# Differential attention with score products over 128 rows, gate inputs moved to the last tiles, and half-width query factors in gated linear attention

## The chip, the cores and the metric

The kernel runs on one core of one Trainium2 chip. The metric is the device time in microseconds (us) from launch to end. The engines in the text are TensorE (PE, with its weight loads shown apart as PEld), VectorE (DVE), ScalarE (ACT), GpSimd (POOL) and SyncE (SP, which here only issues DMAs).

## The reference

Four mixers run one after the other on a sequence of 1024 positions and 1024 features: gated linear attention (GLA), a dilated sliding-window attention, differential attention (DA), and a latent attention (MLA). The change touches the first and the third.

In GLA (4 heads, 128 key and 256 value features per head) the attention inside a chunk is a product of queries and keys with a decay that depends on both positions:

```
diff  = bc[:, :, :, None, :] - bc[:, :, None, :, :]
decay = where(causal, exp(where(causal, diff, 0.0)), 0.0)
att   = einsum('bhid,bhjd,bhijd->bhij', qc, kc, decay)
```

In DA each of 8 heads has two score maps (c = 0, 1) with 64 features each, whose softmaxes are subtracted; the values have 128 features. The result is normalised, multiplied with a gate made from z (the "gate inputs", a quarter of the input projection) and projected:

```
sc = einsum('bqhcd,bkhcd->bhcqk', qb, k) * scale
p  = softmax(sc, axis=-1)
p  = p[:, :, 0] - lam * p[:, :, 1]
o  = einsum('bhqk,bkhd->bqhd', p, v)
...
o  = rmsnorm(o, subln_g) * (1.0 - lambda_init)
o  = o.reshape(b, s, DA_WIDTH) * silu(z)
return o @ w_out
```

## The kernel before

Products in full precision are made from three passes: each operand is split into a rounded part (hi) and a remainder (lo), and hi·hi, lo·hi and hi·lo are added in PSUM (the lines L165, L166 and L167 of one helper). Each product has 128x128 weights and up to 512 moving columns.

**Filler.** The independent projections are cut into *units* with *pieces*; a piece of the width met here is three products of 512 columns. A `Fill` object holds the queue. `fill.give(ns)` issues pieces at this place of the program until their estimated cost has used up the credit, `fill.need(tag)` issues until a unit is complete, `fill.keep` is the number of pieces that `give` must leave over, and what is left at the end of a stage (`self.left`) is issued in the boundary that follows. So the order on TensorE is fixed when the program is written; an engine waits in its own order.

**GLA.** `gla_core` runs over the 4 heads. For each level m in 64, 32, .. 1 the pairs of positions that straddle a block border of size m get their decay: VectorE writes the exponents e for both halves (L478, L479; 512 columns each), ScalarE applies exp to all 1024 columns, VectorE multiplies the keys (L482, tile `ktl`, two buffers) and the queries (L483, in place into e), and TensorE multiplies the two in 128x128 blocks (L495 for m below 64, L487 for m = 64; both in unsplit fp32, which the trace shows as two passes for each product). L496 copies the valid parts into `att` under a mask; then a `give` follows.

**DA.** The body runs over 64 tiles i of 128 queries (8 heads of 8 tiles). At tile i TensorE transposes the tile of j = i - 2 (`attend`, L1248), whose evacuation is split into PTh (ScalarE, L1250) and PTl (VectorE); then come the 8 score products of tile i (L1443, into the PSUM tile `sc` with two buffers, one for each c, both of two banks); then, after odd j, the norm of the pair of tiles before (L161), filler by `give`, and the value products `pv` of the pair (L1381, L1382, L1384; L1379 transposes the row sums). The two maps of a tile go through a maximum on VectorE (L1447) and an exp on ScalarE (L1449); `combine` (L1465 to L1467) subtracts them one tile later.

The operands of the scores are made by filler units `u_k` and `u_q` of the next head, with their rotation on GpSimd and VectorE. `QS[c]` holds the hi part of the queries in its 64 rows and the lo part in the other 64; `KH[c]` holds the hi part of the keys in both halves (L1346 by ScalarE, L1347 a second cast on GpSimd); `KL` holds lo parts. A product over all 128 rows (QS with KH) gives hi·hi + lo·hi; a product over 64 rows (QS with KL) gives hi·lo. The order is: for c = 0 both 128-row products, both 64-row ones; for c = 1 both 64-row ones, then both 128-row ones.

**Gate inputs.** `zs` holds 13 units of 8 pieces (a head and a half of the sequence each). Two are issued before the body, one is added at the start of each of the heads 0 to 6 and three at head 7; the last one is added behind the loop with keep = 8, so that its pieces stand in the boundary. There, per head and half of the sequence, `gated` loads z (L793), the attention output (L794) and the norm factors (L802) by SP's queue, and makes the left operands `oh` and `ol` of the output projection (L796 to L804).

Of the kernel before, what the change touches and what calls it, by code (L numbers as in the profile page):

```python
# [137 lines left out]
class Kern:  # L138
# [317 lines left out]
    def gla_core(self, gp, pp, fill, h, qT, kT, v, bs, masks, ahead):  # L456
# [14 lines left out]
        for li, m in enumerate(LEVELS):  # L471
# [11 lines left out]
            V.tensor_tensor(e, qT, e, op=OP.mult)  # L483
            if m == 64:
                pl = pp.tile([128, 8, 64], F32, name="lv")
                for c in range(8):
                    T.matmul(pl[:64, c, :], kt_[:, c * 128:c * 128 + 64], e[:, c * 128 + 64:c * 128 + 128], start=True, stop=True)  # L487
                V.tensor_copy(att[:64].rearrange("p (c i) -> p c i", i=128)[:, :, 64:128], pl[:64])
                fill.give(2200)
                continue  # L490
            for hf in range(2):
                pl = pp.tile([128, 512], F32, name="lv")
                for c in range(4):
                    cc = slice((4 * hf + c) * 128, (4 * hf + c) * 128 + 128)
                    T.matmul(pl[:, c * 128:c * 128 + 128], kt_[:, cc], e[:, cc], start=True, stop=True)  # L495
                V.copy_predicated(view(att[:, half(hf)])[:, :, 1, :],  # L496
                                  masks[:, li * 256:li * 256 + 256].rearrange("p (n m) -> p n m", m=m), view(pl)[:, :, 1, :])
# [755 lines left out]
    def factors(self, pool, hs):  # L1253
# [3 lines left out]
        t, e, y = (lambda x: (x[:, 0], x[:, 1], x[:, 2]))(pool.tile([128, 3, 4 * len(hs)], F32, name="vr"))  # L1257
# [23 lines left out]
    def da(self, before):  # L1281
# [3 lines left out]
        with ExitStack() as ctx:  # L1285
# [34 lines left out]
            QS, KH, KL, VH = {}, {}, {}, {}  # L1320

            def u_q(h):
                def pre():
                    QS[h] = [dp.tile([128, 1024], F32R, name=f"qs{c}", bufs=2) for c in range(2)]

                def evac(hf, s, ps):
                    def rest(t1, t2):
                        (G if h else V).tensor_tensor(t1, t1, t2, op=OP.add)
                        for c in range(2):
                            a, b = rows[c], rows[1 - c]  # L1330
                            S.copy(QS[h][c][a, s], t1[a])
                            self.lo(G if h else V, QS[h][c][b, s], t1[a], QS[h][c][a, s])
                    return self.rope(None, ps, C, Sn, s, self.SWAP64, rest, 0.125, ((dp, 2),) * 2 if hf else None)
                return self.u_t(("q", h), ("da_wq", h), evac, pre=pre)

            def u_k(h):
                def pre():
                    KH[h] = [dp.tile([128, 1024], F32R, name=f"kh{c}", bufs=2) for c in range(2)]
                    KL[h] = dp.tile([128, 1024], F32R, name="kl", bufs=2)

                def evac(hf, s, ps):
                    def rest(t1, t2):
# [462 lines left out]
```

## Time and profile before

| what | before |
|---|---|
| median of 3 runs (lowest to highest) | 2756.11 us (2754.12 to 2759.56) |
| the profiled execution | 2754.68 us |
| its span, first to last instruction | 2752.9 us |
| PE busy | 2651.4 us (96%) |
| DVE busy | 1873.2 us (68%) |
| ACT busy | 1337.4 us (49%) |
| POOL busy | 312.7 us (11%) |

The span is 1.8 us shorter than the profiled execution's own time; the rest lies around it. In the span the stages follow each other: GLA's cores lie between about 40 and 380 us, the body of DA between about 1470 and 1982 us, and the boundary between DA and MLA begins at about 1983 us. PE and PEld are the same engine: a weight load can run while the product before it still streams. A matmul's duration in the trace runs from its start to its modelled end and overlaps with the next; what a product costs in a stream is the distance between starts.

### The profile page before, as it was taken

To read this page: it belongs to the slowest core of one execution; us is meant where nothing else is said; L and a number is where in the kernel's file an instruction comes from. 1 tells how busy PE (TensorE), PEld (TensorE's weight loads), DVE (VectorE), ACT (ScalarE), POOL (GpSimd) and SP (SyncE) were. 2 spreads that over 40 slices of the span, in tenths; PEclk is the share of its full clock that TensorE was granted. 3 is DMA by queue.
4 is the path that set the end of the run, shared out by engine and by line. 5 is a ranking of instruction groups with operands and counts; after the bars stand their busy time and mean duration, and the time that the engine had idled before them with its cause. 6 is when DMAs were issued, how large, how long until landed. Compare 5 with 4: busy or idle time off the path is not lost.

```text
span 2752.9 us, 39334 instructions
## 1 busy us (share of the span) xinstructions
PE 2651.4 (96%) x14804; PEld 2232.2 (81%) x14804; DVE 1873.2 (68%) x3431; ACT 1337.4 (49%) x2530; POOL 312.7 (11%) x224
## 2 busy tenths in 40 slices
PE   8999999999999999989999999999899999999998
PEld 7889887887778878867787787777678788888878
DVE  7776637657666666666657878888776527777785
ACT  5543344415343434445615676666545424555562
POOL 0000000000000000000005666666100000000000
PEclk9999999999999999999999999999999999999999
DMA  5311146554111111154553222222375220100143
GB/s 207 108 41 37 47 149 205 202 190 147 51 50 47 41 48 47 57 175 158 193 195 90 58 60 69 63 68 54 97 278 173 75 76 24 30 28 30 38 174 111
DMA packets 155606, 274.70 MB, mean 100 GB/s; under 512 B 24564, under 2 KB 74068, under 8 KB 153752
## 3 DMA queue, kind: packets, MB, share of 16 engines
q1 hardware_dynamic: 155416, 272.19, 30.1%
q8 instruction: 116, 1.90, 0.3%
q14 instruction: 74, 0.61, 0.1%
HBM read 195.48 MB, written 66.17 MB: 95 GB/s over the span
## 4 chain that ended last, share of the span: by engine, by line
PE 70%; DVE 14%; DMA 7%; ACT 5%; issue 3%; SPq 1%; POOL 0%; DVEq 0%; ACTq 0%; POOLq 0%
PE mm L165 15%; PE mm L166 15%; PE mm L167 15%; PE pt L1248 3%; PE sc L1443 3%; PE sc L1681 2%; PE sc L1057 2%; PE lv L495 1%; DVE den L1447 1%; DVE P L1467 1%; PE pt L1161 1%; DVE wlo L150 1%; PE mm L1647 1%; PE sc L166 1%; ACT P L1449 1%
## 5 line engine op out<-in xcount | busy, mean ns | idle before, releaser
L165 PE MATMUL mm<-xh,whi 128*128 128x512 f32 x1456 | 611.2, 420 | 8.0 <-DVE t L919 4.3
L167 PE MATMUL mm<-xh,wlo 128*128 128x512 f32 x1456 | 573.5, 394 | 2.0 <-POOL wlo L150 2.0
L166 PE MATMUL mm<-xl,whi 128*128 128x512 f32 x1456 | 573.4, 394 | 1.7 <-DVE xl L150 1.7
L165 PEld LDWEIGHTS mm<-xh,whi 128*128 128x128 f32 x1456 | 276.9, 190 | 64.8 <-DVE t L919 5.6
L167 PEld LDWEIGHTS mm<-xh,wlo 128*128 128x128 f32 x1456 | 275.4, 189 | 62.8 <-POOL wlo L150 2.7
L166 PEld LDWEIGHTS mm<-xl,whi 128*128 128x128 f32 x1456 | 276.7, 190 | 52.6 <-DVE xl L150 4.1
L150 POOL TENSOR_TENSOR wlo<-wraw,whi 128x1024 fp32r<-128x1024 f32 x29 | 70.2, 2422 | 1322.1 <-ACT whi L192 1320.4
L165 PE MATMUL mm<-wvhi,xh 128*128 128x256 f32 x704 | 206.6, 293 | 6.2 <-DVE v L349 2.0
L192 ACT CAST whi<-wraw 128x1024 fp32r<-128x1024 f32 (+2 forms) x141 | 136.0, 964 | 135.9 <-PE mm L166 126.9
L167 PE MATMUL mm<-wvhi,xl 128*128 128x256 f32 x704 | 201.1, 286 | 0.0
L166 PE MATMUL mm<-wvlo,xh 128*128 128x256 f32 x704 | 200.7, 285 | 0.0
L1449 ACT ACTIVATE P<-sc,den 128x1024 f32<-128x1024 f32 x128 | 142.8, 1116 | 109.6 <-DVE den L1447 109.5
L150 DVE TENSOR_TENSOR wlo<-wraw,whi 128x1024 fp32r<-128x1024 f32 (+2 forms) x113 | 123.6, 1093 | 88.2 <-ACT whi L192 81.3
L1447 DVE TENSOR_REDUCE den<-sc 128x1 f32<-128x1024 f32 x128 | 153.0, 1211 | 0.7 <-PE sc L1443 0.7
L165 PEld LDWEIGHTS mm<-wvhi,xh 128*128 128x128 f32 x704 | 136.2, 194 | 11.5 <-ACT vs L1297 4.4
L1051 ACT ACTIVATE P<-P,nm 128x128 f32<-128x128 f32 (+1 forms) x192 | 84.9, 443 | 124.3 <-DVE nm L1049 124.0
L166 PEld LDWEIGHTS mm<-wvlo,xh 128*128 128x128 f32 x704 | 136.9, 194 | 1.0 <-issue 0.7
L167 PEld LDWEIGHTS mm<-wvhi,xl 128*128 128x128 f32 x704 | 136.2, 193 | 0.0
L165 PE MATMUL mm<-oh,xh 128*128 128x512 f32 (+1 forms) x336 | 126.0, 375 | 0.6 <-ACT oh L804 0.5
L166 PE MATMUL mm<-ol,xh 128*128 128x512 f32 (+1 forms) x336 | 123.9, 369 | 2.2 <-DVE ol L150 2.2
L167 PE MATMUL mm<-oh,xl 128*128 128x512 f32 (+1 forms) x336 | 123.4, 367 | 0.0
L1061 DVE CUSTOM_DVE_ANT_0 P<-sc,band 128x128 f32<-128x128 f32 (+1 forms) x192 | 59.6, 348 | 70.0 <-PE sc L1057 69.4
(352 smaller groups left out, 6086.2 us busy)
## 6 DMA issues: line engine op xcount, KB each, us to landing
xa<-in_ada_w SPq DMA_DIRECT2D x12, 2048.0 KB
d_z<-zt SPq DMA_DIRECT2D x64, 256.0 KB
oh<-d_z SPq DMA_DIRECT2D x64, 256.0 KB
ol<-d_o SPq DMA_DIRECT2D x64, 256.0 KB
d_r<-X SPq DMA_DIRECT2D x48, 256.0 KB
wraw<-in_swa_wq SPq DMA_DIRECT2D x24, 512.0 KB
res<-d_r SPq DMA_DIRECT2D x40, 256.0 KB
zt<-zt SPq DMA_DIRECT2D x160, 64.0 KB
```

The source lines that it names most:

```text
L150: eng.tensor_tensor(out, src, hi.bitcast(F32), op=OP.subtract)
L165: mm(ps, l[0], r[0], start=first, stop=False)
L166: mm(ps, l[0], r[1], start=False, stop=False)
L167: mm(ps, l[1], r[0], start=False, stop=last)
L192: nc.scalar.copy(hi, raw)
L1051: S.activation(p[:, off:off + w_], p[:, off:off + w_], AF.Exp, bias=nm[:, g, b:b + 1], scale=scale, accum_out=stat(h, g, 1, b))
L1057: T.matmul(sc[:, b % 2, :w_], q[:, b * 128:b * 128 + 128], k[:, k0:k0 + w_], start=True, stop=True)
L1061: V.tensor_tensor_reduce(p[:, off:off + w_], sc[:, b % 2, :w_], mk, 1.0, NEG, op0=OP.add, op1=OP.max, accum_out=stat(h, g, 0, b))
L1248: nc.tensor.transpose(pt[:, i, :], P[:, (4 * j + i) * 128:(4 * j + i) * 128 + 128], self.ident)
L1443: T.matmul(sc[c][:, s], QS[h][c][r, q0:q0 + 128], (KL[h] if k else KH[h][c])[r, s], start=first, stop=not first)
L1447: V.tensor_reduce(dn[:, 2 + c:3 + c], sc[c], AX, OP.max, negate=True)
L1449: S.activation(p, sc[c], AF.Exp, bias=dn[:, 2 + c:3 + c], accum_out=dn[:, 1:2] if c else d0)
```

## The change

In GLA the query factor is made only for the second half of each block, into a tile `eq` of 512 columns (two tiles, `khT` and `qh`, in turn), and a product has 64 moving columns in place of 128. One PSUM tile per level takes all eight products.

In DA `QH[c]` holds the hi part of the queries in both halves of the rows and `KK[c]` the keys' hi part in its 64 rows and lo part in the other 64. `QL` (a ring of three half tiles for each c, of which GpSimd clears the unused rows once) holds the lo part of the queries in 64 rows and zeros in the others. QH with KK gives hi·hi + hi·lo, QL with KK gives lo·hi. All eight products of a tile run over 128 rows. For keys two casts per half of the sequence on GpSimd are gone, for queries two casts on ScalarE are new. The value halves are split from a buffer of their own instead of `vr`, and the norm factors take a `kh` buffer.

The gate inputs are taken in another order; the body adds one unit at each even head and four at head 7, and the last three units (24 pieces) are added at j = 62 with keep = 11. The credits in the body change with it.

```diff
@@ gla_core
-            V.tensor_tensor(e, qT, e, op=OP.mult)
+            eq = gp.tile([128, 512], F32, name=("khT", "qh")[li % 2])
+            V.tensor_tensor(eq.rearrange("p (n m) -> p n m", m=m), view(qT)[:, :, 1, :], ev[:, :, 1, :], op=OP.mult)
...
+            pl = pp.tile([128, 512], F32, name="lv")
+            for c in range(8):
+                T.matmul(pl[:, c * 64:c * 64 + 64], kt_[:, c * 128:c * 128 + 128], eq[:, c * 64:c * 64 + 64], start=True, stop=True)
             for hf in range(2):
-                pl = pp.tile([128, 512], F32, name="lv")
-                for c in range(4):
-                    cc = slice((4 * hf + c) * 128, (4 * hf + c) * 128 + 128)
-                    T.matmul(pl[:, c * 128:c * 128 + 128], kt_[:, cc], e[:, cc], start=True, stop=True)
@@ da
+            QL = [[dp.tile([128, 512], F32R, name=f"ql{c}{i}") for i in range(3)] for c in range(2)]
+            for i in range(3):
+                for c in range(2):
+                    G.memset(QL[c][i].bitcast(F32)[rows[1 - c], :], 0.0)
... u_q
-                            S.copy(QS[h][c][a, s], t1[a])
-                            self.lo(G if h else V, QS[h][c][b, s], t1[a], QS[h][c][a, s])
+                            S.copy(QH[h][c][a, s], t1[a])
+                            self.lo(G if h else V, QL[c][(2 * h + hf) % 3][a, :], t1[a], QH[h][c][a, s])
+                            S.copy(QH[h][c][b, s], t1[a])
... u_k
-                            S.copy(KH[h][c][a, s], t1[a])
-                            (G if h else V).tensor_copy(KH[h][c][b, s], t1[a])
-                            self.lo(G if h else V, KL[h][a, s], t1[a], KH[h][c][a, s])
+                            S.copy(KK[h][c][a, s], t1[a])
+                            self.lo(G if h else V, KK[h][c][b, s], t1[a], KK[h][c][a, s])
... load_v
-                vr = dp.tile([128, 8, 128], F32, name="vr")
+                vr = vl.bitcast(F32)
...
-                  [(hf, h) for h in range(3, 8) for hf in range(2)]]
+                  [(hf, h) for h in range(3, 6) for hf in range(2)] + [(0, 6), (0, 7), (1, 6), (1, 7)]]
... the body
+                if j == 62:
+                    fill.add(*zs)
+                    fill.keep = 11
...
-                        for _ in range(1 if h < 7 else 3):
+                        for _ in range(4 if h == 7 else 1 - h % 2):
                             fill.add(zs.pop(0))
...
-                    for n, (c, hf, k) in enumerate(((0, 0, 0), (0, 1, 0), (0, 0, 1), (0, 1, 1), (1, 0, 1), (1, 1, 1), (1, 0, 0), (1, 1, 0))):
-                        mm(c, hf, k, (c, hf) not in seen)
+                    scores(0)
+                    exps(0)
+                    scores(1)
...
-                    fill.give(4000 if j > 55 else 4200 if j > 7 else 4250)
+                    fill.give(4500 if j > 61 else 3200 if j > 55 else 4000 if j > 7 else 4250)
                 elif j >= 0 and j % 2:
-                    fill.give(2200 if j > 55 else 2300 if j > 7 else 2040)
+                    fill.give(4500 if j > 61 else 1700 if j > 55 else 2200 if j > 7 else 2040)
...
-            fill.keep = 8
-            fill.add(*zs)
+            fill.give(2500)
             norm(*nrm)
```

**TensorE at the last two score tiles.** The rows are in program order: line, operation, target from its two sources (kh, kl: keys; qs, ql: queries; the number is a buffer), shape and count. Before:

```order
L1384 MATMUL mm<-PTl,vh 128x256 x8
L1248 MATMUL pt<-ident,P 128x128 x8
L1443 MATMUL sc<-kh_16598,qs_16607 128x512 x2
L1443 MATMUL sc<-kl,qs_16607 128x512 x2
L1443 MATMUL sc<-kl,qs_16608 128x512 x2
L1443 MATMUL sc<-kh_16599,qs_16608 128x512 x2
L1248 MATMUL pt<-ident,P 128x128 x8
```

With the change, in the same place, the first of the filler pieces that now follow the eight products included:

```order
L1393 MATMUL mm<-PTl,vh 128x256 x8
L1250 MATMUL pt<-ident,P 128x128 x8
L1457 MATMUL sc<-kh_16498,qs_16506 128x512 x2
L1457 MATMUL sc<-kh_16498,ql_12401 128x512 x2
L1457 MATMUL sc<-kh_16499,qs_16507 128x512 x2
L1457 MATMUL sc<-kh_16499,ql_12404 128x512 x2
L165 MATMUL mm<-xh_70,whi 128x512
L166 MATMUL mm<-xl_72,whi 128x512
L167 MATMUL mm<-xh_70,wlo 128x512
```

The products of c = 0 and c = 1 stand in the same order of keys (hi with lo, then again), and five pieces stand before the next transposes, where none stood.

**TensorE behind the last scores.** Before, from the value products of the last pair but one to those of the last:

```order
L1384 MATMUL mm<-PTl,vh 128x256 x8
L1248 MATMUL pt<-ident,P 128x128 x8
L161 MATMUL mm<-sq_17838,ones_r 128x256
L161 MATMUL mm<-sq_17839,ones_r 128x256
L1248 MATMUL pt<-ident,P 128x128 x8
L1379 MATMUL mm<-ident,dsum 4x128
```

With the change, up to the first piece there:

```order
L1393 MATMUL mm<-PTl,vh 128x256 x8
L1250 MATMUL pt<-ident,P 128x128 x8
L161 MATMUL mm<-sq_17764,ones_r 128x256
L161 MATMUL mm<-sq_17765,ones_r 128x256
L165 MATMUL mm<-xh_70,whi 128x512
L166 MATMUL mm<-xl_72,whi 128x512
L167 MATMUL mm<-xh_70,wlo 128x512
```

Seven pieces now stand between this norm and the last transposes and seven more between those and the last value products; behind the last norm stand 11 pieces, where 8 stood. Counted over the whole stage, 332 pieces are issued in either kernel; up to tile i = 60 it is 304 before and 277 with the change, and at the tiles 61 to 65 it is 0, 0, 0, 0, 0 before and 2, 5, 3, 7, 7 with the change.

## Rows read from the trace of the kernel before

**Rows 1.** The page, busy time: engine, us, share of the span, instructions.
```profile
PE 2651.4 (96%) x14804; PEld 2232.2 (81%) x14804; DVE 1873.2 (68%) x3431; ACT 1337.4 (49%) x2530; POOL 312.7 (11%) x224
```
**Rows 2.** Windows: length, each engine's busy us, clock, DMA share, GB/s.
```profile
1480.00:1968.00 488.00, 480.53 (x2699) 382.39 (x2698) 401.44 (x492) 330.70 (x631) 283.08 (x200) 1.00 0.22 62
1949.00:1991.40 42.40, 31.46 (x173) 24.94 (x171) 28.34 (x60) 23.96 (x49) 2.80 (x3) 0.92 0.27 76
1991.40:2016.00 24.60, 22.11 (x80) 16.90 (x81) 22.93 (x48) 14.04 (x21) 0.00 (x0) 0.86 1.03 367
```
**Rows 3.** Timeline of PE in GLA: start, us, operation, count [idle before].
```profile
59.81 1.15 PE L487 MATMUL lv<-e,ktl 128*64 128x64 f32 x16
313.81 1.95 PE L495 MATMUL lv<-e,ktl 128*128 128x128 f32 x16
```
**Rows 4.** Timeline of weight loads in the sliding-window stage.
```profile
704.77 0.58 PEld L1117 LDWEIGHTS sc<-xb,sel 128*128 128x128 f32 x4 [3.72 <-DVE xb L1108]
```
**Rows 5.** Line L483: its durations (ns), and who waited for it (us, times).
```profile
L483 DVE TENSOR_TENSOR e<-qT,e x28: 1211/1216/1255, 55.0 to 337.5; 128x1024 f32<-128x1024 f32 x28
...
  PE lv L495: 5.8, 6
```
**Rows 6.** Groups in 1480 to 1968 us: busy us, mean ns, idle before.
```profile
L1347 POOL CAST kh<-zt 64x512 fp32r<-64x512 f32 x28 | 22.3, 798 | 1.5
L1331 ACT CAST qs<-zt 64x512 fp32r<-64x512 f32 x28 | 17.3, 616 | 9.7 <-POOL zt L1328 9.4
L1447 DVE TENSOR_REDUCE den<-sc 128x1 f32<-128x1024 f32 x127 | 151.9, 1211 | 0.7 <-PE sc L1443 0.7
L1467 DVE SCALAR_TENSOR_TENSOR P<-P,den 128x1024 f32<-128x1024 f32 x63 | 101.3, 1608 | 2.1
L150 DVE TENSOR_TENSOR PTl<-pt,PTh 128x512 fp32r<-128x512 f32 x124 | 81.5, 679 | 6.1 <-ACT PTh L1250 6.1
```
**Rows 7.** Timeline of PE: two tiles' scores and what follows them; the first one's c = 1 waits.
```profile
1668.80 0.73 PE L1443 MATMUL sc<-kl,qs 64*128 64x512 f32 x2 [0.30 <-ACT P L1449]
...
1670.03 0.40 PE L161 MATMUL mm<-sq,ones_r 128*128 128x256 f32 x2
...
1944.80 0.71 PE L1443 MATMUL sc<-kh,qs 128*128 128x512 f32 x2
1945.44 0.74 PE L1443 MATMUL sc<-kl,qs 64*128 64x512 f32 x4
...
1946.67 0.39 PE L165 MATMUL mm<-xh,whi 128*128 128x512 f32 x1
```
**Rows 8.** Line L1443: idle time before it, until whom (us, times).
```profile
  ACT P L1449: 11.8, 18
```
**Rows 9.** Timeline of PE in MLA: a score block behind transposes.
```profile
2301.27 0.71 PE L1681 MATMUL sc<-kp,qp 128*128 128x512 f32 x2
...
2302.51 0.62 PE L1681 MATMUL sc<-kp,qp 128*128 128x512 f32 x2
```
**Rows 10.** Timeline of PE behind tile 61: waits, and one filler piece.
```profile
1957.73 1.07 PE L1248 MATMUL pt<-ident,P 128*128 128x128 f32 x8 [1.02 <-DVE den L1465]
...
1963.30 0.73 PE L1443 MATMUL sc<-kh,qs 128*128 128x512 f32 x2 [1.83 <-ACT P L1449]
...
1974.74 1.82 PE L1248 MATMUL pt<-ident,P 128*128 128x128 f32 x8 [1.50 <-DVE PTl L150]
...
1981.74 0.39 PE L161 MATMUL mm<-sq,ones_r 128*128 128x256 f32 x1 [1.36 <-ACT sq L154]
...
1982.77 0.39 PE L165 MATMUL mm<-xh,whi 128*128 128x512 f32 x1
...
1983.45 0.39 PE L165 MATMUL mm<-xh,whi 128*128 128x512 f32 x1
...
1991.40 0.50 PE L165 MATMUL mm<-oh,whi 128*128 128x512 f32 x1 [3.03 <-ACT oh L804]
```
**Rows 11.** The chain that ended last, in the boundary: start, us, what.
```profile
2002.54 6.11 DMA rsb<-d_rs
```

More of the change, by code (lines that the diff above doesn't have):

```diff
@@ L486, in gla_core @@
                 for c in range(8):
-                    T.matmul(pl[:64, c, :], kt_[:, c * 128:c * 128 + 64], e[:, c * 128 + 64:c * 128 + 128], start=True, stop=True)
+                    T.matmul(pl[:64, c, :], kt_[:, c * 128:c * 128 + 64], eq[:, c * 64:c * 64 + 64], start=True, stop=True)
                 V.tensor_copy(att[:64].rearrange("p (c i) -> p c i", i=128)[:, :, 64:128], pl[:64])
@@ L1436, in da, with scores @@
                     sc = [None] * 2
-                    def mm(c, hf, k, first):
-                        s = half(hf)
-                        if sc[c] is None:
-                            sc[c] = pp.tile([128, 1024], F32, name="sc", bufs=2)
-                        r = rows[c] if k else slice(0, 128)
-                        T.matmul(sc[c][:, s], QS[h][c][r, q0:q0 + 128], (KL[h] if k else KH[h][c])[r, s], start=first,
-                                 stop=not first)
+                    def scores(c):
+                        sc[c] = pp.tile([128, 1024], F32, name="sc", bufs=2)
+                        ql = QL[c][(2 * h + t // 4) % 3][:, t % 4 * 128:t % 4 * 128 + 128]
+                        for k in range(2):
+                            for hf in range(2):
+                                T.matmul(sc[c][:, half(hf)], ql if k else QH[h][c][:, q0:q0 + 128], KK[h][c][:, half(hf)], start=k == 0,
+                                         stop=k == 1)
                     def exps(c):
@@ L1450, in exps @@
                         P.append(p)
-                    seen = set()
-                    for n, (c, hf, k) in enumerate(((0, 0, 0), (0, 1, 0), (0, 0, 1), (0, 1, 1), (1, 0, 1), (1, 1, 1), (1, 0, 0), (1, 1, 0))):
-                        mm(c, hf, k, (c, hf) not in seen)
-                        seen.add((c, hf))
-                        if n == 3:
-                            exps(0)
+                    scores(0)
+                    exps(0)
+                    scores(1)
+                    done[0] = i + 1
                     if nrm and j % 2:
```

38 lines of the change are left out of this document (20 added, 18 removed).

## The prediction

> **What bounds the kernel now.** The page's busy times come first: TensorE is busy 96% of the span [rows 1], so time falls only where TensorE has less to issue, or where it now waits. The windows tell the three places apart [rows 2]. In the body of DA (1480 to 1968 us) it is busy 480.5 of 488.0 us at full clock, VectorE 401, ScalarE 331 and GpSimd 283: filler covers nearly every wait. From 1949 to the first product of the boundary at 1991.4 it is busy 31.5 of 42.4 us at a clock of 0.92. Here the filler has run out, and the list of TensorE's waits [rows 10] shows what it waits for: the chain exp, combine, transposes, split, value products, norm. In the boundary the DMAs are full (1.03, 367 GB/s), and the chain goes through a norm factor that arrives 6.1 us after its predecessor [rows 2, 11]. So filler in the body costs its full length, and in the tail only what it exceeds the waits by. My sum is made against the profiled execution, 2754.7 us; the median of the runs is 1.4 us above it, and I add that at the end.
>
> **GLA.** A level below 64 has 16 passes (eight products in two) which take 1.95 us [rows 3], 15 distances and one duration of 0.28 us, thus 0.11 us a pass. Halving the moving columns would halve that if the columns set the pace. They don't: in the sliding-window stage, four products with 32 moving columns and the same 128 weight columns have four weight loads in 0.58 us [rows 4], three distances of about 0.11 us and one load of about 0.25. So I cost the narrower products at nothing (bounds 0 and the gain of the last rival below). What goes is a wait: TensorE stood 5.8 us in 6 places for the query factor [rows 5], a VectorE operation of 1.22 us on 1024 columns. On 512 columns it takes about 0.68, which the 128x512 subtraction of PTl (0.68 us, the same engine and width) bears out [rows 6]. It is also written to a tile of its own, so that the next level's factor no longer stands behind this level's use of e. If only the shorter duration counted, 6 x 0.54 = 3 us would go, less where the exp then comes last; at best all 5.8 and the fringe. I take **-5.8** (-2 to -7). VectorE loses 28 x 0.54 = 15 us there, which elsewhere was cover.
>
> **DA's operands.** For keys 28 casts of 0.80 us leave GpSimd (22.3 us); for queries 32 casts of 0.62 us come to ScalarE, +20 us on 331 of 488 [rows 2, 6]. They are pieces of work for the next head, and filler covers waits of ScalarE while it lasts: 0 here, bound by rival two. The six clearings run on GpSimd ahead of the body, where it has nothing else. At the start of the body the split of weights and the first operands stand on VectorE and GpSimd; two casts less may shorten that by **-1** (-2 to 0). The load of values now goes to a buffer that the value products of the head before read last. If that made SP wait, the weight loads and the row exchange of the rotation behind it in SP's queue would wait too; it is issued at a head's fifth tile, more than 20 us after that last reader, so 0.
>
> **DA's scores.** The eight products of a tile take 1.87 us (1944.80 to 1946.67), in 45 of 64 tiles within 0.03 of that. The 64-row products of c = 0 and c = 1 run in pairs, four of them in the 0.74 us of one row [rows 7]. All the same eight cost eight times 0.23, for those before and behind stand 0.31 to 0.34 apart. With 128 rows throughout, MLA shows what a block behind transposes costs: five products in 1.24 us [rows 9], that is 0.31 for the first and 0.23 for each that follows. Eight then cost 0.31 + 7 x 0.23 = 1.93, +0.05 x 64 = +3.2. Against that stand the 18 waits for the buffer of c = 1 (the exp two tiles of scores before, 11.8 us) [rows 8]. In such a tile nothing overlaps, and the last four products take 1670.03 - 1668.80 = 1.23 us [rows 7]; in the new form 4 x 0.23 = 0.92. That is 0.31 x 18 = -5.6. Together **-2.4** (-6, where the waits go too, to +3, where the gain does not come).
>
> **Moved filler.** Counted from the program, 304 pieces stood up to tile 60 and 277 do now. A piece, three products, takes 1983.45 - 1982.77 = 0.68 us [rows 10], so the body loses 27 x 0.685 = -18.5, in full, since it is busy throughout. Of these, 24 (16.4 us) now stand at tiles 61 to 65, and three in the boundary, where TensorE waits 3.03 us in any case [rows 10]. The tail has 42.40 - 31.46 - 3.03 = 7.9 us of waits and runs at 0.92, which is 0.08 x 42.4 = 3.4 us of slow clock, 11.3 in all [rows 2]. Of the waits, those before the transposes (1.02, 1.50) and before the last scores (1.83) have pieces ahead of them now: 4.35 us. Those before the norms stay (1.36 is the longest), since no piece stands between the value products and the norm. The clock fell towards its lower level behind these waits; with them filled I count that time as won, 3.4. Absorbed 4.35 + 3.4 = 7.75, added 16.4: +8.6. Together -18.5 + 8.6 = **-9.9** (-13.4, where all 11.3 are absorbed, to -2, where nothing is).
>
> **The boundary and the body's thin places.** Eleven pieces instead of eight hold a weight buffer longer, so one more load of 512 KB falls into the stretch where the DMAs are full: 512 KB at 367 GB/s is 1.4 us [rows 2], **+1.4** (0 to +3). The credits leave three and no pieces, or five and none, at the tile pairs 14/15, 30/31 and 46/47. There VectorE has, for each of the two tiles, two maxima, a subtraction and two splits, 2 x 1.21 + 1.61 + 2 x 0.68 = 5.4 us [rows 6], 10.8 for the pair, against 10.5 to 12 of TensorE. I take **+1.5** (0 to +4).
>
> Sum: -5.8 - 1 - 2.4 - 9.9 + 1.4 + 1.5 = **-16.2**, which is 2738.5 against the profiled execution and 2739.9 against the median.
>
> **The rivals.** *The tail does not absorb.* VectorE is busy 28.3 and ScalarE 24.0 of the tail's 42.4 us; if their chain simply starts later by each piece, because transposes stand behind pieces in TensorE's order, the tail grows by all 16.4: 2739.9 + 7.8 = 2748. Against it: the pieces stand in front of waits on just that chain [rows 10]. *ScalarE's new casts delay the exps.* 32 x 0.62 = 20 us in full: 2760. For it, exps gate both `sc` buffers [rows 8]; against it, ScalarE is free for a third of the body [rows 2]. *Slower: weight loads come to light.* If a 128-row product behind a 128-row product with other weights waits for its load, as inside the old block (0.33 from start to start), a block costs 8 x 0.33 = 2.65: 64 x 0.77 = +49 and the -2.4 is lost, 2792. The kernel gets slower from a block of 1.88 + 13.8/64 = 2.09 us. MLA's five in 1.24 us speak against it [rows 9]. The Trainium skill would have it so (TensorE: Matmul & The Clock Gate, Part 3: Packing small matmuls): weight loads overlap a running matmul only where its row group differs, and 128-row products use all groups; MLA's rows do not agree with that. *GLA's products do halve.* A pass with 64 weight columns and 64 moving ones costs (1.15 - 0.14) / 16, about 0.06 us [rows 3]; were that the price here, 24 levels x 16 x 0.05 = 20 us more go: 2720. The Trainium skill says in the same page, section Back-to-back issue gap, that the distance follows the moving columns down to a floor, which speaks for it; its section on LDWEIGHTS lets the load follow the weight's columns, and our rows 4 are on that side.
>
> **How the numbers follow.** The forecast, 2733 to 2746, has a chance of 0.70; no absorption 0.11; casts 0.07; slower 0.05; halved products 0.07. The range from 2731 to 2751 holds the first two and leaves out 0.19. A measurement here can tell about 0.2%, 5.5 us, from no change: below 2750.6 is faster. Faster are the forecast, the halved products and most of the tail's case, 0.84; the casts and the tail's worse end are about the same, 0.09; slower 0.07, the loads with a little of the casts.
>
> **What would show it.** Passes of the GLA lines still 0.11 us apart and no wait there for the query factor; a score block of 1.93 us at nearly all tiles; TensorE busy at full clock up to the last norm, with waits only before norms; the stretch from the transposes of tile 61 to the last norm longer by about 8 us, and the body before it shorter by some 22. I would be wrong if VectorE or GpSimd turned out to set the pace of the body once filler is thinner (then pairs of tiles last as long as before, with TensorE idle in them), or if the boundary's loads, which start after the last norm, were held up by more than one weight load.

## The result: slower, 2778.2 us

The changed kernel takes 2778.19 us (median of 4 runs, 2774.75 to 2780.48), against 2757.36 for the kernel before in the same comparison: a ratio of 1.008 with a 95% interval of 1.0067 to 1.0093, 22 us. The prediction was 2740 with a range up to 2751, and faster. Below, a time difference against the kernel before is its ratio less 1 times 2755 us, since several comparisons were made and each has its own runs of the kernel before; the intervals are about 3 us to either side, and so 4 to 5 us for the difference of two such figures. Lengths of stages come from one traced execution each: where the code is the same, the body of DA repeats within 1.3 us, while the stretch from GLA's last level product to the body took from 1127.3 to 1133.9 us in two runs that do not differ there.

### The profile page after: what moved, and what is told of

The parts are those of the page before. It is cut to its first block, busy times and chain, and to the rows that moved or that the text cites. A ratio compares the mean times of both kernels' runs of the same rounds, so it can differ in the third digit from the quotient of the medians.

```text
span 2775.2 us, 39339 instructions
## 1 busy us (share of the span) xinstructions
PE 2657.9 (96%) x14804; PEld 2262.3 (82%) x14804; DVE 1859.0 (67%) x3427; ACT 1357.0 (49%) x2562; POOL 295.9 (11%) x202
## 5 line engine op out<-in xcount | busy, mean ns | idle before, releaser
L150 POOL TENSOR_TENSOR wlo<-wraw,whi 128x1024 fp32r<-128x1024 f32 x29 | 77.5, 2671 | 1356.5 <-ACT whi L192 1353.9
L165 PEld LDWEIGHTS mm<-wvhi,xh 128*128 128x128 f32 x704 | 136.6, 194 | 11.9 <-ACT vs L1299 4.1
```

Of the source, the lines that this page charges most:

```text
L150: eng.tensor_tensor(out, src, hi.bitcast(F32), op=OP.subtract)
L165: mm(ps, l[0], r[0], start=first, stop=False)
```

## The profile after

The windows of the body, the tail and the start of the boundary in the changed kernel (length, busy time of PE, PEld, DVE, ACT and POOL, granted clock, DMA share, GB/s) answer to [rows 2]:

```profile
1480.00:1968.00 488.00, 463.83 (x2590) 393.07 (x2589) 389.01 (x481) 337.21 (x641) 256.18 (x168) 0.99 0.20 57
1953.00:2008.00 55.00, 49.85 (x267) 41.58 (x266) 36.18 (x72) 29.53 (x57) 11.18 (x8) 0.97 0.30 88
2008.00:2035.00 27.00, 20.58 (x78) 14.62 (x77) 23.05 (x48) 14.19 (x21) 0.00 (x0) 0.96 1.03 372
```

TensorE is now idle 24 of 488 us in the body, where it was idle 7.5. The body became as long as before with less to do. From the first score product of tile 0 to that of tile 60 it took 1944.80 - 1470.94 = 473.9 us before and takes 1953.00 - 1475.83 = 477.2 now. The timeline of PE at these places (before, then after):

```profile
1470.94 0.61 PE L1443 MATMUL sc<-kh,qs 128*128 128x512 f32 x2
```

```profile
1475.83 0.62 PE L1457 MATMUL sc<-kh,qs 128*128 128x512 f32 x2
...
1953.00 0.71 PE L1457 MATMUL sc<-kh,qs 128*128 128x512 f32 x2
```

What TensorE waited for there (engine, line, whom it waited for: us in total, times, longest), before from 1470 to 1945 us, then after from 1475 to 1953, and last what ScalarE waited for after, from 1470 to 1945:

```profile
PE mm L167 <- POOL wlo L150: 2.0, 1, 2.0
PE sc L1443 <- ACT P L1449: 1.6, 5, 0.4
PE pt L1248 <- DVE PTl L150: 1.4, 2, 1.1
PE mm L1384 <- DVE PTl L150: 1.0, 1, 1.0
```

```profile
PE sc L1457 <- ACT P L1463: 8.3, 9, 2.0
PE mm L1390 <- ACT zt L925: 6.8, 2, 3.4
PE mm L1393 <- DVE PTl L150: 2.8, 4, 1.0
PE mm L165 <- ACT y L1395: 2.6, 3, 1.6
```

```profile
ACT vh L1366 <- DMA vl<-d_v: 11.0, 6, 2.8
```

Nearly all the new waits of TensorE are for ScalarE, and ScalarE has a wait that is not among those of before: the cast of the next head's values (L1366) stands in its queue before the values have arrived, six times in the body, 11.0 us. One of the six, from ScalarE's timeline:

```profile
1686.97 1.04 ACT L1366 CAST vh<-vl 128x1024 fp32r<-128x1024 f32 x1 [2.84 <-DMA vl<-d_v]
1687.92 1.11 ACT L1463 ACTIVATE P<-sc,den 128x1024 f32<-128x1024 f32 x1
...
1694.09 1.11 ACT L1463 ACTIVATE P<-sc,den 128x1024 f32<-128x1024 f32 x1 [2.48 <-DVE den L1461]
...
1696.13 0.58 ACT L925 COPY zt<-mm 128x512 f32<-128x512 f32 x1
```

SP issued the load that this cast waits for at 1682.64, 4.3 us ahead of the cast's start. Before, the load had a buffer of its own, `vr`, which GpSimd freed at once, and SP issued it a head ahead, as SP's and ScalarE's timelines of the kernel before show for one head:

```profile
1682.64 0.58 SPq L1365 DMA_DIRECT2D vl<-d_v  x1
```

```profile
1619.81 0.58 SPq L1354 DMA_DIRECT2D vr<-d_v  x1
...
1675.95 1.04 ACT L1357 CAST vh<-vr 128x1024 fp32r<-128x1024 f32 x1
```

It had 56 us to land. With the change the load goes into `vl`, which the value products of the head before last still read. In the trace the loads for the heads 2 to 7 are issued between 0.3 and 5.3 us after the last of these products, and the cast, which needs `vh` from the same products, stands 4.3 to 4.6 us behind the issue. One such pair, the load for head 5, on TensorE and on SP's queue:

```profile
1743.94 0.28 PE L1391 MATMUL mm<-PTh,vl 128*128 128x256 f32 x1
```

```profile
1744.25 0.58 SPq L1365 DMA_DIRECT2D vl<-d_v  x1
```

What the 2.84 us set off is seen on TensorE and VectorE: the exp at 1687.92 is late, `combine` is late (and takes 2.41 us, where [rows 6] have a mean of 1.61), the next maximum is late, ScalarE waits for that at 1694.09, and its copy at 1696.13 frees a PSUM bank for which the value products stand 3.38 us:

```profile
1689.17 0.73 PE L1457 MATMUL sc<-kh,qs 128*128 128x512 f32 x2 [2.02 <-ACT P L1463]
...
1696.77 0.39 PE L1390 MATMUL mm<-PTh,vh 128*128 128x256 f32 x1 [3.38 <-ACT zt L925]
...
1698.76 0.41 PE L1390 MATMUL mm<-PTh,vh 128*128 128x256 f32 x1
1698.98 0.41 PE L1391 MATMUL mm<-PTh,vl 128*128 128x256 f32 x1
```

```profile
1690.51 2.41 DVE L1478 SCALAR_TENSOR_TENSOR P<-P,den 128x1024 f32<-128x1024 f32 x1
```

The first products behind the wait of 3.38 us go 0.12 us from start to start (1697.82 to 1697.94), those from 1698.3 on 0.21: the granted clock had fallen to 0.50, the lower of its two levels (1.2 GHz), as the window shows (length, busy times, clock, DMA share, GB/s):

```profile
1698.30:1701.50 3.20, 3.20 (x17) 3.20 (x16) 2.34 (x3) 0.36 (x1) 1.04 (x2) 0.50 0.45 109
```

Tile 27, in which this stands, takes 16.1 us; the same tile took 7.85 before.

In GLA the waits for the query factor are gone, and two others have come (TensorE's waits, 40 to 345 us); the kernel before has the second with 1.5 us and not the first:

```profile
PE o L538 <- DVE st L542: 3.4, 1, 3.4
PE ms L555 <- DVE sq L553: 3.1, 1, 3.1
```

The score block is as forecast, 1976.73 - 1974.81 = 1.92 us against the 1.87 of [rows 7]:

```profile
1974.81 0.71 PE L1457 MATMUL sc<-kh,qs 128*128 128x512 f32 x2
...
1976.73 0.40 PE L161 MATMUL mm<-sq,ones_r 128*128 128x256 f32 x2
```

## The experiments

First each part of the change alone. GLA alone (`eq` and products of 64 columns, L483 to L497):

> The kernel before with the GLA part of the change alone (query factor on 512 columns in the tiles khT and qh, products of 64 moving columns); DA and its filler as before. The trace of the changed kernel lost the waits for the query factor there and had new ones (3.4 us for a state update queued behind the scan of the next head, 3.1 us for a square sum). Theory: this part alone costs +2 to +4 us, 2758 to 2760. Rival, the new waits belong to the filler's position and not to this part: -4 to -6 us, 2750 to 2752. In both, the passes of the level products stay about 0.11 us apart.

Measured 2751.39 us, ratio 0.9994 (0.9983 to 1.0006). The median lies in the rival's range; the ratio, 1.7 us less with an interval from 4.7 less to 1.7 more, shows neither the loss nor the gain. The rival's reason falls all the same: the trace has the same two new waits (3.3 and 3.1 us), so they belong to this part.

The moved gate inputs alone:

```diff
+                if j == 62:
+                    fill.add(*zs)
+                    fill.keep = 11
...
-                        for _ in range(1 if h < 7 else 3):
+                        for _ in range(4 if h == 7 else 1 - h % 2):
```

> The kernel before with the movement of the gate inputs alone (order of units, one at each even head and four at head 7, 24 pieces at j = 62, keep = 11, the new credits); scores and value loads as before, so the values are still loaded a head ahead. Theory loads (the body's new waits come from value loads that are no longer ahead): the body loses 15 to 19 us, the tail gains some 10 and the boundary 2 to 4, together -3 to -7, 2749 to 2753. Theory thin (the body's waits come from the missing filler itself): the body loses at most 5 us, together +7 or more, 2763 and above.

Measured 2762.65, ratio 1.0031 (1.0019 to 1.0043), +8.5 us: the time of theory thin, with a body between the two. Here the values are loaded a head ahead, and still the body is only 473.9 - 465.2 = 8.7 us shorter with 28 pieces fewer. (The trace counts 300 pieces from tile 0 to tile 60 before and 272 after; the program's 304 and 277 of the prediction took in neighbouring tiles.)

The operands and scores of DA alone:

> The kernel before with the DA operands and scores of the change alone (128-row products, ring of QL, casts moved from GpSimd to ScalarE, values loaded into the buffer vl, norm factors in a kh buffer); filler and GLA as before. Theory loads: ScalarE stands 1.4 to 2.8 us at each of 7 value loads, and filler covers a part of it on TensorE: +2 to +8 us, 2758 to 2764. Theory thin: with the old filler nothing shows, -2 us, 2754. In both, a score block takes 1.93 us at nearly all tiles.

Measured 2759.74, ratio 1.0017 (1.0007 to 1.0026), +4.7 us, in the range of theory loads. The trace bears it out only in part: the body is 3.4 us longer (477.2), the tail behind tile 60 is 3.0 us shorter (33.9 for 36.9), and 5.7 us lie ahead of the body, where runs with the same code differ by as much. The three parts alone make -1.7 + 8.5 + 4.7 = +11.5 us, together they made 22: they get into each other's way.

Then the suspected causes in the changed kernel, one by one. The load two tiles earlier in the program (a new function `fetch_v` at the third tile of a head):

> The changed kernel, with the DMA of the next head's values issued two tiles earlier (at the third tile of a head instead of the fifth; the casts stay). Theory loads: ScalarE no longer waits for these loads (14.0 us in 8 in the changed kernel), the two stretches around 1689 and 1817 us lose 5 us of waits each and some slow clock behind them, together -11 to -16 us against the changed kernel, 2762 to 2767. Theory thin: the waits stay under other names, at most -4 us, 2774 or more.

Measured 2776.27, ratio 1.0079 (1.0064 to 1.0094). This run told nothing of the two theories: the load kept its place in SP's queue, at 1681.52 us, and ScalarE waited as before. Moving the load in the program did not move it in SP's queue: here too it stands 0.3 to 5.1 us behind the last product that reads the buffer, so there was little room ahead of it.

Without the loads:

```diff
-                vr = vl.bitcast(F32)
-                nc.sync.dma_start(vr, self.vd[h // 2][:, :, (h % 2) * 128:(h % 2) * 128 + 128])
+                vr = C.rearrange("p (k n) -> p k n", n=128)
```

> The changed kernel without the DMAs of the values in DA: vh and vl are made from the resident rotation table C, at the same places and by the same engines. It leaves out the loads of v, so DA's values are wrong data; the time shows what waiting for the loads costs. (In the run with the load two tiles earlier the DMA kept its place in SP's queue, ScalarE still waited 11.1 us in 6 for it, so that run told nothing of the loads.) Theory loads: the long tiles 27 and 43 (7 and 8 us over what their pieces need) shrink to under 3, in all -8 to -12 us against the changed kernel, 2766 to 2770. Theory thin (too little filler in heads 1, 3 and 5): they stay above 5, in all -3 us at most, 2775.

Measured 2761.44, ratio 1.0026 (1.0014 to 1.0038): +7.2 us instead of +22, so 15 us hang on these loads, more than the 8 to 12 expected. Tiles 27 and 43 lose 6 to 6.5 us each.

The queries' second copies on GpSimd:

```diff
-                            S.copy(QH[h][c][b, s], t1[a])
+                            (G if h else V).tensor_copy(QH[h][c][b, s], t1[a])
```

> The changed kernel with the second copies of the queries' hi part (2 casts per half, 28 in the body) made by GpSimd in place of ScalarE. Theory casts (ScalarE's queue delays the exps): ScalarE loses 17 us in the body, the body gets 5 to 10 us shorter, 2768 to 2773. Theories loads and thin: ScalarE waits, it does not lack time, so within 3 us of the changed kernel, 2775 to 2781, longer if GpSimd slows VectorE.

Measured 2768.5, ratio 1.0054 (1.0037 to 1.0071), 7 us better than the changed kernel, as theory casts had it; the casts looked like a cause of their own. Tiles 27 and 43 stayed long. The run with all three mends, below, says otherwise.

Gate units at each head:

```diff
-                        for _ in range(4 if h == 7 else 1 - h % 2):
+                        for _ in range(1 if h < 7 else 4):
```

> The changed kernel with one gate unit at each of the heads 0 to 6 and four at head 7, nothing added at j = 62 (credits and keep as in the change). In program order 294 pieces stand up to tile 60 (300 before, 272 with the change) and no tile of heads 1, 3 and 5 is without pieces. Theory thin: the time beyond what the pieces need, 25 us in the heads 1, 3 and 5 of the changed kernel, falls to about 5; 22 pieces come back to the body (+15), the tail and boundary give back about as much as they took over (-8 to -12): in all -11 to -17 us, 2761 to 2767. Theory loads: the excess at tiles 27 and 43 stays, in all -2 us or more, 2776 or above.

Measured 2766.7, ratio 1.0046 (1.0031 to 1.0061), in time what theory thin expected, but not by its reason. The body did not get shorter: with 22 pieces more it takes 485.4 us, 8.2 more than with the change, and tile 19, where a value load falls, is now the long one (16.6 us). What was gained lies behind the body, where 14 pieces fewer stand up to the last norm (38.8 us for 47.3) and 8 fewer behind it (285.8 us to MLA's first scores, for 291.0).

The same hold-back with the old scores, and GLA:

> The kernel before with the GLA part, and the even hold-back of the run with one unit at each head (294 pieces up to tile 60, 15 in the tail, 3 in the boundary), with the old operands and scores and the values loaded a head ahead. If the tail's waits (4.35 us before transposes and scores and 3.4 us of slow clock) take the 11 pieces that come to it, and the boundary does not need its 8 pieces, the body gains 6 x 0.685 = 4.1 and the GLA part its 2 to 3: 2748 to 2752, against 2755 for the kernel before. If the tail takes none of it: 2756 or more.

Measured 2760.49, ratio 1.0027 (1.0016 to 1.0038), 9 us slower than GLA alone. With only six pieces fewer the body lasted 480.3 us instead of 472.6 with all. The values are loaded a head ahead here, so the hold-back costs by itself.

The next four mend the causes. Value casts later in ScalarE's queue:

```diff
-                S.copy(vh, vr)
+                with tc.issue_after(EX[-1].ins) if EX else ExitStack():
+                    S.copy(vh, vr)
...
+                    if t == 6 and h < 7:
                         load_v(h + 1)
...
-                        S.activation(p, sc[c], AF.Exp, bias=dn[:, 2 + c:3 + c], accum_out=dn[:, 1:2] if c else d0)
+                        EX.append(S.activation(p, sc[c], AF.Exp, bias=dn[:, 2 + c:3 + c], accum_out=dn[:, 1:2] if c else d0))
```

> The changed kernel, complete, with ScalarE's cast of the next head's values put behind the exps of a head's sixth tile, a tile or more later in ScalarE's queue than in the changed kernel; the loads stay where they are. Theory loads (the loss is not the load but that ScalarE's queue stands behind it): ScalarE's 11 us of waits for it vanish, tiles 27 and 43 fall to under 2.5 us beyond their pieces, in all -10 to -16 us against the changed kernel, 2762 to 2768. Rival, the run without loads was shorter because 7 x 512 KB less were moved: no more than -3 us, 2775.

Measured 2766.73, ratio 1.0035 (1.0022 to 1.0048): 12 us better than the changed kernel, with all the loads there. The rival (fewer bytes) falls. Of ScalarE's waits for the loads 1.1 us in one is left, ahead of the body:

```profile
L1375 ACT CAST vh<-vl x8: 1036/1039/1052, 1448.3 to 1893.5; 128x1024 fp32r<-128x1024 f32 x8
...
  DMA vl<-d_v: 1.1, 1
```

All three mends:

> The changed kernel with three mends: value casts later in ScalarE's queue, the queries' second copies on GpSimd, and the query factor of GLA in a tile of its own (by the order of VectorE's instructions, the state update again stands ahead of the next head's scan). If the three causes add up (loads 14, casts 8, GLA 4): 2752. If loads and casts were the same slack of ScalarE won twice: 2758 to 2762.

Measured 2758.45, ratio 1.0004 (0.9995 to 1.0013), the second of the two expectations.

GLA alone with a tile of its own:

```diff
-            eq = gp.tile([128, 512], F32, name=("khT", "qh")[li % 2])
+            eq = gp.tile([128, 512], F32, name="eq")
```

> The kernel before with the GLA part alone, the query factor in a tile of its own in place of khT and qh. If the shared tiles caused the new waits (3.3 us for the state update, 3.1 for the square sum), both go and the part brings the 5 to 6 us that it took from the waits for the query factor: 2749 to 2751 where the kernel before takes 2755. If not, as the run with the shared tiles, 2752 to 2756.

Measured **2743.17, ratio 0.9953 (0.994 to 0.9965)**: 12.9 us faster than the kernel before, 7 us more than expected, and with the next run the fastest of all. From the first to the last product of L495 the trace gains 5.9 us; the rest lies in steps of 1 to 3 us ahead of that and up to the sliding-window stage. The one ahead (2.7 us up to the first level product) is not the change's: the runs with GLA as before take 57.3 to 59.8 us for it. The others were not tracked down. VectorE's timelines around the state update, with the shared tiles (after) and with the own one, show what the name of a tile did:

```profile
109.16 2.63 DVE L453 TENSOR_TENSOR_SCAN b<-ones_r,la 128x128 f32<-128x128 f32 x8
111.71 0.46 DVE L542 SCALAR_TENSOR_TENSOR st<-st,dec,ms 128x256 f32<-128x256 f32 x1
```

```profile
103.52 0.47 DVE L542 SCALAR_TENSOR_TENSOR st<-st,dec,ms 128x256 f32<-128x256 f32 x1
103.91 2.63 DVE L453 TENSOR_TENSOR_SCAN b<-ones_r,la 128x128 f32<-128x128 f32 x8
```

With the shared tiles the state update L542 stands behind eight scans of the next head, and TensorE 3.4 us behind it; with a tile of its own it stands ahead of them, and these waits are 1.1 and 1.5 us.

GLA with its own tile and the new scores (the scores run below):

> The kernel before with the GLA part in a tile of its own and with the change's DA operands and scores, value casts later in ScalarE's queue, filler as before. What the 128-row scores cost by themselves: 64 x 0.05 = 3 us in the body, so 2752 to 2755; if the saved waits for the score buffer pay for that, as predicted, 2746 to 2749.

Measured 2743.94, ratio 0.9952 (0.9938 to 0.9965): by the time, the scores neither cost nor bring anything that these intervals can tell. In the trace the body takes 471.5 us, against 473.0 without them, and the tail from tile 60 to the last norm 33.8 against 37.1. The body's gain lies in its first two tiles (13.3 us for 15.1), at the start that the prediction had at -1.

What was open then was the filler. The next two take pieces from the body without leaving a tile dry:

> The kernel of the scores run with GLA in a tile of its own (value casts later), with one gate unit at each of the heads 0 to 6, four at head 7, and the change's credits: 294 pieces up to tile 60 (300 in the scores run, 272 with the change), no tile of the body without pieces, but 8 to 9 pieces at once at the starts of later heads. Theory dry tiles (the body does not get shorter with fewer pieces only where a tile has none): the time beyond the pieces stays at the 9.4 us of the scores run, within 3, so the body gets 6 x 0.685 = 4 us shorter. Theory pace (the other engines need the time wherever pieces are taken): it rises by 4 or more, the body gains nothing, and the total is 2 or more us above the 2743.9 of the scores run.

Measured 2753.82, ratio 0.9998 (0.9988 to 1.0008), 12.7 us worse than the scores run. Next the credits a little below the old ones (and keep = 8 instead of 11):

```diff
-                    fill.give(4500 if j > 61 else 3200 if j > 55 else 4000 if j > 7 else 4250)
+                    fill.give(4500 if j > 61 else 3200 if j > 55 else 4150 if j > 7 else 4250)
...
-                    fill.give(4500 if j > 61 else 1700 if j > 55 else 2200 if j > 7 else 2040)
+                    fill.give(4500 if j > 61 else 1700 if j > 55 else 2270 if j > 7 else 2040)
```

> As the run with one unit at each head, but with credits only a little below the old ones (4150 and 2270): 295 pieces up to tile 60, never less than 6 and 3 nor more than 7 and 4 in a tile. Theory dry tiles: as that run, the body 3.4 us shorter than in the scores run. Theory pace: no shorter. If this one is shorter and the other is not, the bursts of 8 to 9 pieces at head starts are what costs.

Measured 2747.32, ratio 0.9974 (0.9965 to 0.9984), 6 us worse than the scores run. Neither gains, so dry tiles are not the whole cause. Theory pace is not shown either: engines that need their time wherever pieces are taken can keep the body from getting shorter, but both bodies got longer, 480.1 and 477.7 us with 294 and 295 pieces against 471.5 with 300. The smoother one loses less. What both traces have, and the scores run has not, are waits of TensorE for a bank of `mm`; the next section comes back to them. Two lines of the first of these runs and one of the second, over their bodies:

```profile
PE mm L165 <- ACT sq L1419: 4.1, 3, 1.5
PE mm L1399 <- ACT zt L927: 3.0, 3, 1.0
```

```profile
PE mm L1397 <- ACT zt L925: 4.3, 3, 2.4
```

The last run leaves the copies of the queries on ScalarE:

> The changed kernel with value casts later and GLA's query factor in a tile of its own, the queries' second copies on ScalarE as in the change. Against the run with all three mends this tells what the copies cost when ScalarE no longer waits for loads: equal to it (2758 within 3) if the copies mattered only through that wait; 5 or more us longer (2763 and above) if they cost by themselves.

Measured 2756.54, ratio 1.0007 (0.9998 to 1.0017), equal to the run with all three mends within the intervals: the copies on ScalarE cost nothing that can be told once it no longer waits for loads.

## What the body costs besides its filler

In the traces, tile 0 to tile 60, with 0.685 us to a piece [rows 10]:

| kernel | time, us | pieces | time less 0.685 for each piece |
|---|---|---|---|
| before | 473.9 | 300 | 268.4 |
| GLA own tile, new scores | 471.5 | 300 | 266.0 |
| the same, 295 pieces, evenly | 477.7 | 295 | 275.6 |
| the same, 294 pieces, in bursts | 480.1 | 294 | 278.7 |
| new scores alone, value casts as in the change | 477.2 | 300 | 271.7 |
| GLA with shared tiles, old scores, 294 pieces | 480.3 | 294 | 278.9 |
| changed, one unit at each head | 485.4 | 294 | 284.0 |
| moved gate inputs alone | 465.2 | 272 | 278.9 |
| changed, own tile, casts later | 468.2 | 272 | 281.9 |
| changed, no value loads | 467.6 | 272 | 281.3 |
| changed | 477.2 | 272 | 290.9 |

The last column is what the tiles cost beyond filler. With the old placing of pieces it is 266 to 268, whichever scores are used, as long as no cast waits for its load; with the value casts of the change it is 6 more. With any other placing it is 276 and more, and the value loads put 9 on top. TensorE's waits, from about tile 0 to tile 60, in the run with own tile and scores (before) and in the one that also moves the gate inputs:

```profile
PE sc L1464 <- ACT P L1470: 2.7, 3, 1.0
PE pt L1250 <- DVE PTl L150: 2.3, 6, 0.8
PE mm L1402 <- DVE PTl L150: 0.9, 1, 0.9
```

```profile
PE pt L1250 <- DVE PTl L150: 7.1, 5, 3.0
PE sc L1468 <- ACT P L1474: 4.2, 7, 1.0
PE mm L1399 <- ACT zt L925: 2.7, 2, 1.4
PE mm L1402 <- DVE PTl L150: 2.0, 3, 1.0
```

6 us of waits have become 16 and more: the splits, exps and copies between two products take the time that the pieces covered.

Between these two kernels 28 pieces go, 19.2 us, and the body gets 3.3 us shorter; compared tile by tile, 9.1 of the missing 15.9 us lie at the three pairs that have hardly any filler now. Tiles 14/15, 30/31 and 46/47 lose 7, 5 and 5 pieces and take 15.6, 14.3 and 14.5 us, where they took 15.9, 15.7 and 15.4. Their windows (length, busy time of PE, PEld, DVE, ACT and POOL, granted clock, DMA share, GB/s):

```profile
1572.98:1588.56 15.58, 12.62 (x71) 10.75 (x69) 14.20 (x16) 12.64 (x26) 11.70 (x8) 0.89 0.20 59
1699.62:1713.90 14.28, 12.93 (x77) 10.71 (x75) 11.65 (x15) 12.35 (x25) 11.49 (x7) 1.00 0.18 46
1824.17:1838.70 14.53, 12.55 (x77) 10.57 (x75) 13.79 (x16) 12.87 (x26) 11.40 (x7) 1.00 0.16 42
```

VectorE is busy 14.20, 11.65 and 13.79 us of them (13.19, 13.22 and 12.38 in the scores run, with all pieces) and ScalarE 12.64, 12.35 and 12.87; no run tells which of the two sets the pace. That is the prediction's own sign of being wrong: pairs that last nearly as long as before, with TensorE idle in them.

The other tiles lose 11 pieces (7.5 us) and get 0.7 us shorter. Part of what they lose is waits for a bank of `mm`. Filler units, norms and value products take the two banks of that PSUM tile in turn, and the next user waits until ScalarE has copied the last result out. In the body of the kernel before and of the scores run these waits sum to 0.1 us or less; with the gate inputs moved alone they are 9.3 of 18.2 us of idle time, in one tile of each of the heads 1 to 6; in the runs with 294 and 295 pieces with GLA's own tile they are 11.9 of 18.1 and 6.5 of 14.0. In the kernel before, a head's units have 40 pieces and so have its tiles, so that units end at the same places in every head. That they end elsewhere in the other kernels, where ScalarE is late with the copy, is a reading of the traces; no run tested it by itself.

## Why the prediction was wrong

The five steps in a row, each kernel against the one ahead of it: GLA with an own tile -12.9; new scores, value casts later -0.3; gate inputs moved +15.1; the factor in `khT` and `qh` +7.7; value casts where the change has them +12.4. The sum is +22.0. Each step is known within 4 to 5 us.

**GLA, forecast -5.8.** The mechanism held with a tile of its own: 5.9 us in the stage, 12.9 in all. The step that failed was "written to a tile of its own": I read two names in turn as tiles of their own, but they are the tiles of the state stage, and with them VectorE's order changed; the order with the state update behind the scan could be read ahead. The step of +7.7 lies in this stage: from the first to the last level product the run with the casts later takes 283.7 us with the shared tiles and 275.8 with the own one (281.8 before). The duration was right: the factor takes 0.685 us on 512 columns, where I had 0.68. So was the step on the passes: 16 passes with 64 columns take 1.90 us, against the 1.95 of [rows 3], so the rival of halved products falls.

```profile
332.02 1.90 PE L495 MATMUL lv<-khT,ktl 128*128 128x64 f32 x16
```

**The value loads, forecast 0.** This is the second step that failed: "more than 20 us after that last reader, so 0". I asked whether SP would wait for the buffer, and found 20 us of room by the program's order; the trace has 0.3 to 5.3 us, at a head's second or third tile. I did not ask when the load had been issued before (56 us ahead), how long it takes to land (over 4 us), and who stands in the queue behind the cast that needs it: the exps. SP's waits for the buffer are 0.9 us in all; it is ScalarE's queue that stood, behind the cast. It cost 12.4 us, 15 by the run without loads.

**ScalarE's casts, forecast 0**, with a rival at +20: right, as the last run shows, though one run seemed to give them 7 us. A reading that fits both, not shown by a run, is that work taken from ScalarE made up for a part of what its queue lost to the loads.

**Scores, forecast -2.4**: right in the block and not refuted in the time, where the step is -0.3 within 4 to 5 us. The block is 1.92 us, and all 64 blocks of a trace together (first product to what follows) go from 132.5 us before to 130.4 in the scores run. The body gains 1.5 us by the scores, at its start, and the tail 3.3. The slower rival, weight loads that come to light, did not happen: products over 128 rows, with a weight load each, start 0.23 us apart (eight in 1.92 us).

**Moved filler, forecast -9.9.** This is the third step, and the largest: "the body loses 27 x 0.685 = -18.5, in full, since it is busy throughout". With all else mended the body lost 471.5 - 468.2 = 3.3 us. A TensorE that is busy 98% of the time says that the filler covers the waits, not that there are none behind it. The row that spoke against it stood in the prediction: ScalarE 331, VectorE 401 and GpSimd 283 of 488 us [rows 2], in a chain. The term for thin places was +1.5 with a bound of +4, from 10.8 us of VectorE's work in a pair. At the three pairs it is 9.1, with VectorE busy for up to 14.2: in the first pair one subtraction of `combine` took 3.39 us where I had 1.61, and work on the next head's operands, which I had left out, stands there too. The remaining 6.8 us lie at tiles that I had not looked at.

The tail was nearer, in part by luck: from the first scores of tile 60 to the last norm's first product it took 1981.74 - 1944.80 = 36.9 us before [rows 7, 10] and 2000.26 - 1953.00 = 47.3 after, +10.3 where I had +8.6. But the new scores alone make it 3.0 to 3.3 us shorter, and the moved pieces 13.5 longer (33.8 to 47.3, own tile and casts later in both). By the trace 25 pieces came to it, 17.1 us, so 3.6 were absorbed where I had 7.75; with the scores alone the wait of 1.50 us before transposes [rows 10] and half of the slow clock had gone already. Body and tail together are 10.2 us longer by the moved pieces, where -9.9 was forecast. TensorE's waits there before the norms stayed, as forecast, and the clock is 1.00 up to the last norm.

```profile
2000.26 0.39 PE L161 MATMUL mm<-sq,ones_r 128*128 128x256 f32 x1 [1.36 <-ACT sq L154]
```

**The boundary, forecast +1.4.** From the last norm to the first scores of MLA it got 3.7 us longer. The chain there again goes through the norm factors (answering to [rows 11]); in the other runs the same stretch varied from -3 to +6 us. It goes with the pieces that stand behind the last norm: 284 to 286 us with two or three (four runs), 286 to 290 with eight (five), 288 to 293 with eleven (eight). Up to the first product of the boundary it is 10 to 11 us with any number, so the pieces themselves are hidden, as forecast, and the cost comes behind them; by what, is open. Two pieces of its chain in the changed kernel (start, us, what):

```profile
2010.32 6.62 DMA rsb<-d_rs
2023.36 6.51 DMA rsb<-d_rs
```

What stays open: which engine sets the three thin pairs, how much of the time lost outside them is the place where units end, why the gain of GLA's own tile is larger than what its stage shows, and the boundary.

## What to carry to other kernels

Filler that covers a stage is worth its length only as far as no wait stands behind it: before moving it, add up what one step of the other engines' chain takes with the filler gone, and expect the time there. Units that end at other places ask for their PSUM banks at other times; look who has to copy them out then. When a buffer is shared or dropped, look at what had been running ahead because of it: find when its load was issued and how long it takes, and who queues behind the first instruction that needs it. A tile's name is a dependency; a new use of an old name can turn the order of an engine that neither use mentions.

## What the runs showed of the hardware

A wait of TensorE can cost more than its length: behind the 3.38 us at 1696.77, products went at 0.21 instead of 0.12 us from start to start, at a granted clock of 0.50 from 1698.3 to 1701.5. It does not have to: around a wait of 2.55 us at 1709.70 in the first run with 294 pieces and own tile the granted clock stayed at 1.00 (1704 to 1717 us). In GLA from 40 to 130 us the granted clock was 0.94 in the changed kernel and 1.00 with the own tile (windows of the two). In the run of GLA alone, with the same code and waits there as the changed kernel, it was 0.98, so the waits are not all of it:

```profile
40.00:130.00 90.00, 83.48 (x527) 75.08 (x526) 62.81 (x106) 42.75 (x57) 0.00 (x0) 0.94 0.32 108
```

```profile
40.00:130.00 90.00, 85.15 (x560) 76.12 (x559) 67.64 (x113) 45.03 (x62) 0.00 (x0) 1.00 0.33 115
```

A load of 512 KB took over 4 us from its issue to the start of the instruction that waited for it, with the DMAs at 0.20 of their time.
